# Dilated attention: the combination of the groups in five steps, each tied to a row minimum of the next items

## The chip, the cores and the metric

The kernel runs on one core of a Trainium2 chip. The metric is the device time of one execution in microseconds (us). The engines are TensorE (PE: matmuls and transposes), VectorE (DVE), ScalarE (ACT) and GpSimd (POOL); DMAs are issued from SyncE's queue (SP). Each engine takes its instructions in the order of its queue, and waits at one whose inputs or buffers are not ready.

## The reference, cut to what matters

The block has three attention mixers, whose outputs are gated, projected and merged. The change is in the first, dilated attention: 24 heads in three groups of eight, each group with its own window and dilation. Each group gives an output and a log-denominator per position and head, and a softmax over the three groups weighs the outputs:

```python
for gi, (window, dil) in enumerate(A_GROUPS):          # ((128, 1), (512, 4), (2048, 16))
    hs = slice(gi * A_HEADS, (gi + 1) * A_HEADS)
    o_g, lse_g = dilated_window_attention(aq[:, :, hs], ak[:, :, hs], av[:, :, hs], window, dil)
    outs.append(o_g)
    lses.append(lse_g)
wts = jax.nn.softmax(jnp.stack(lses, axis=0), axis=0).astype(dt)
oa = jnp.einsum('gbsh,gbshd->bshd', wts, jnp.stack(outs, axis=0)).reshape(b, s, BRANCH_WIDTH)
```

The sequence has 1024 positions, a head 64 channels.

## The kernel before

**Stages.** After the start come cross-attention, grouped-query attention, dilated attention (about 640 to 1165 us of the profiled span), the merge of the three branches, and the output projection. During the attentions PE also works through dense projections, one unit after the other (two halves of 24 matmuls, lines 143, 145 and 147). `weave` interleaves the matmuls of the attention with those of the units by their estimated costs, and PE's queue holds them as they are written. The other queues, SP's among them, are ordered by the recording layer, by priority and estimated readiness. The attention's instructions get a higher priority (`tc.high_priority`); the combination is traced outside of it.

**An item** is one pair of heads and one group. There are 12, in the order (0,0), (0,1), (0,2), (1,0) and so on; `a_att` computes one, in eight query tiles T = 0 to 7. A tile has these steps:

- scores on PE (line 125), into one of two PSUM banks;
- for each of the two heads the row minimum of the masked, negated scores, on DVE (line 939);
- the exponential on ACT (lines 942, 944, 947), into `pra`;
- two tiles later, the transposes of `pra` on PE (lines 965 and 974), into one of two PSUM banks `tr`, and their copy to `app` on ACT (line 977);
- after each four tiles, the matmuls with v (line 989) and the copy of the output to `og` on ACT (line 998). `og` has four buffers.

Meanwhile the dense units make q, k and v of the item after the next. Of each half of q and k, DVE makes three products with the rotary tables (lines 835 to 837) and POOL their sum (line 838, `rot`); then ACT and DVE split the result into a high and a low part: `aqh` (line 105) and `aql` (line 106) for q, `akh` (line 862) and `akl` (line 863) for k, head by head. POOL also copies edges of v (line 885, `vda`). Each unit's own weights arrive as `wr` (line 114, two buffers) and are split into `wh` on ACT (line 105) and `wl` on DVE (line 106).

**The combination** (`combine`) follows the third item of a pair. The statistics of the three groups were written to DRAM (`std`); two loads bring them back as `cpt` (line 1045). Seven small DVE operations and one exponential (lines 1047 to 1058) make the three weights of each position, `ceg`, which go to DRAM as `wgd` (line 1060). Then, for each group and each half of the positions, a pair of loads broadcasts the weights to 64 partitions each (`wgt`, line 1065, one buffer of 128x512), and DVE multiplies the output with them (line 1069). POOL adds the second and third output to the first (line 1071), and the sum goes to DRAM (`od`, line 1072).

The combinations of pairs 0, 1 and 2 run during the items (1,0), (2,0) and (3,0). That of pair 3 runs at the start of the merge, beside its units (line 1109 scales a unit, lines 1160 to 1163 prepare the gated outputs of the first branch, line 1125 accumulates). The merge loads the combined outputs for its third branch, and broadcasts the denominators of the second branch from DRAM with the same form of load (line 1141, 256 KB each, `gt`).

## Time and profile before

| | us |
|---|---|
| median of three runs | 1549.16 (1545.98 to 1551.1) |
| profiled execution | 1545.69 |
| its span, first to last instruction | 1543.9 |
| wgt loads in it (line 1065) | 48 of 128 KB, issued from 761.9 to 1212.5 |
| products with the weights (line 1069) | 24, median 1.09 each, from 766.2 to 1215.5 |
| additions on POOL (line 1071) | 8, median 2.40 each, from 782.4 to 1216.8 |

The profiled execution is 3.5 us shorter than the median of the runs; durations below come from it. A row of a timeline has the start from the span's start, the duration, the engine, the line, the operation, the tile written and the tiles read, and in brackets how long the engine stood idle before and what ended that. A row of waits has the total, the number of times and the longest.

### The profile page before, as it was taken

To read this page: it belongs to the slowest core of one execution; us is meant where nothing else is said; L and a number is where in the kernel's file an instruction comes from. 1 tells how busy PE (TensorE), PEld (TensorE's weight loads), DVE (VectorE), ACT (ScalarE), POOL (GpSimd) and SP (SyncE) were. 2 spreads that over 40 slices of the span, in tenths; PEclk is the share of its full clock that TensorE was granted. 3 is DMA by queue.
4 is the path that set the end of the run, shared out by engine and by line. 5 is a ranking of instruction groups with operands and counts; after the bars stand their busy time and mean duration, and the time that the engine had idled before them with its cause. 6 is when DMAs were issued, how large, how long until landed. Compare 5 with 4: busy or idle time off the path is not lost.

```text
span 1543.9 us, 20861 instructions
## 1 busy us (share of the span) xinstructions
PE 1497.0 (97%) x7748; PEld 1237.3 (80%) x7748; DVE 977.3 (63%) x1610; ACT 712.1 (46%) x1457; POOL 443.4 (29%) x363
## 2 busy tenths in 40 slices
PE   6999989999999999999999999999999999999998
PEld 5899977777777778888878877887888788888787
DVE  7765469989988975655566566556634442524743
ACT  5443345666677661645545445454643111212321
POOL 4415513454444543211231222123100100222422
PEclk9999999999999999999999999999999999999999
DMA  5342011111111112111120121112125451523432
GB/s 210 96 124 69 29 45 59 54 56 48 62 35 59 62 64 88 38 28 42 58 69 29 42 72 55 42 34 84 37 69 186 149 159 34 193 80 113 126 110 96
DMA packets 56966, 119.81 MB, mean 78 GB/s; under 512 B 14176, under 2 KB 24096, under 8 KB 56736
## 3 DMA queue, kind: packets, MB, share of 16 engines
q1 hardware_dynamic: 56720, 118.34, 23.8%
q8 instruction: 61, 1.00, 0.3%
q14 instruction: 41, 0.34, 0.1%
q10 hardware_dynamic: 144, 0.13, 0.0%
HBM read 96.06 MB, written 22.38 MB: 77 GB/s over the span
## 4 chain that ended last, share of the span: by engine, by line
PE 74%; DVE 12%; DMA 4%; issue 4%; ACT 3%; POOL 2%; SPq 1%; DVEq 0%; POOLq 0%; ACTq 0%
PE d L147 12%; PE d L143 12%; PE d L145 12%; PE sc L125 7%; PE sc L1226 4%; PE s L125 3%; PE sc L147 2%; PE sc L145 2%; PE sc L143 2%; PE ov L989 2%; DMA wgt<-wgd 2%; DVE bpl L106 2%; PE s L709 1%; PE ov L730 1%; PE s L708 1%
## 5 line engine op out<-in xcount | busy, mean ns | idle before, releaser
L143 PE MATMUL d<-hh,wh 128*128 128x512 f32 x992 | 396.0, 399 | 2.4 <-DVE fth L222 2.4
L147 PE MATMUL d<-hh,wl 128*128 128x512 f32 x992 | 397.3, 400 | 0.0
L145 PE MATMUL d<-hl,wh 128*128 128x512 f32 x992 | 393.6, 397 | 0.0
L143 PEld LDWEIGHTS d<-hh,wh 128*128 128x128 f32 x992 | 187.2, 189 | 39.2 <-DVE fth L222 3.2
L147 PEld LDWEIGHTS d<-hh,wl 128*128 128x128 f32 x992 | 187.1, 189 | 39.0 <-issue 4.1
L145 PEld LDWEIGHTS d<-hl,wh 128*128 128x128 f32 x992 | 187.3, 189 | 36.2 <-issue 1.0
L105 ACT ACTIVATE wh<-wr 128x1024 fp32r<-128x1024 f32 (+1 forms) x100 | 95.4, 954 | 242.9 <-PE sc L145 107.6
L838 POOL TENSOR_TENSOR rot<-rot,t2a 128x512 f32<-128x512 f32 x48 | 82.6, 1720 | 313.6 <-DVE t2a L837 313.6
L720 POOL TENSOR_TENSOR bl<-bl,bp 128x512 f32<-128x512 f32 x96 | 135.5, 1412 | 120.4 <-ACT bp L711 112.0
L106 DVE TENSOR_TENSOR bpl<-bp,bph 128x512 fp32r<-128x512 f32 x128 | 130.5, 1020 | 23.8 <-ACT bph L105 23.3
L106 DVE TENSOR_TENSOR wl<-wr,wh 128x1024 fp32r<-128x1024 f32 (+1 forms) x100 | 120.7, 1208 | 21.9 <-ACT wh L105 21.2
L711 ACT ACTIVATE bp<-s 128x512 f32<-128x512 f32 x128 | 76.2, 595 | 60.0 <-PE s L709 58.1
L1128 POOL TENSOR_TENSOR acc<-acc,th 128x1024 f32<-128x1024 f32 x16 | 45.4, 2836 | 192.7 <-DVE th L1127 192.7
L947 ACT ACTIVATE pra<-pra,sts 128x128 f32<-128x128 f32 (+2 forms) x152 | 67.1, 442 | 61.3 <-DVE sts L939 60.6
L147 PE MATMUL sc<-hh,wl 128*128 128x512 f32 x224 | 87.3, 390 | 2.3 <-DVE wl L106 2.3
L691 DVE TENSOR_REDUCE bn<-tr 128x1 f32<-128x512 f32 x128 | 86.6, 680 | 4.4 <-PE tr L690 4.0
L939 DVE CUSTOM_DVE_ANT_0 pra<-s,mask 128x128 f32<-128x128 f32 (+2 forms) x152 | 48.3, 348 | 62.3 <-PE s L125 50.1
L143 PE MATMUL sc<-hh,wh 128*128 128x512 f32 x224 | 87.3, 390 | 0.0
L145 PE MATMUL sc<-hl,wh 128*128 128x512 f32 x224 | 87.1, 389 | 0.0
L105 ACT ACTIVATE bph<-bp 128x512 fp32r<-128x512 f32 x128 | 80.8, 631 | 3.5
L835 DVE TENSOR_TENSOR rot<-d,tab 128x512 f32<-128x512 f32 x48 | 33.1, 690 | 73.3 <-PE d L147 73.1
L125 PE MATMUL sc<-gh,wh 128*128 128x512 f32 x192 | 74.7, 389 | 0.0
(278 smaller groups left out, 3097.2 us busy)
## 6 DMA issues: line engine op xcount, KB each, us to landing
wr<-in_wu SPq DMA_DIRECT2D x76, 512.0 KB
g2d<-fth SPq DMA_DIRECT2D x24, 256.0 KB
wgt<-wgd SPq DMA_DIRECT2D x48, 128.0 KB
ot<-od SPq DMA_DIRECT2D x12, 512.0 KB
gt<-g2d SPq DMA_DIRECT2D x12, 512.0 KB
wr<-in_wbr SPq DMA_DIRECT2D x24, 256.0 KB
thd<-fth SPq DMA_DIRECT2D x20, 256.0 KB
th<-thd SPq DMA_DIRECT2D x10, 512.0 KB
```

The lines of the kernel that those rows point to most:

```text
L105: A.activation(dst_h, src, AF.Copy)
L106: V.tensor_tensor(dst_l, src, dst_h.bitcast(F32), op=OP.subtract)
L125: PE.matmul(out_ps, a, b, start=i == 0, stop=i == n - 1)
L143: PE.matmul(dst, wh[:, k, :], hh[k][:, t], start=k == 0, stop=False)
L145: PE.matmul(dst, wh[:, k, :], hl[k][:, t], start=False, stop=False)
L147: PE.matmul(dst, wl[:, k, :], hh[k][:, t], start=False, stop=k == 7)
L691: V.tensor_reduce(st[i]["n"][:, j, c:c + 1], s, axis=AX.X, op=OP.min)
L711: A.activation(pp, s, AF.Exp, scale=-1.0)
L720: G.tensor_tensor(lsum[i % 2], lsum[i % 2], pp, op=OP.add)
L838: G.tensor_tensor(o[:, t], o[:, t], t2, op=OP.add)
L947: A.activation(src, raw, AF.Exp, scale=-1.0, bias=bias, accum_out=sts[:, h, 1, T:T + 1])
L1226: PE.matmul(parts[h], *terms[h][j], start=j == 0, stop=j == 23)
```

## The change

`combine` no longer issues its work at once. It returns five steps (the loads of the statistics; the weights, with their store and the first broadcast; one weighting per group), which are put on a list. In `a_att` of the following items, after the scores of tile T have been traced, the next step is traced if T is the step's number in `STEP_T`: 0, 2, 4 and 6 of the next item and 1 of the one after. `tc.issue_after` puts the step's DVE instructions behind that tile's last row minimum on DVE's queue; instructions of other engines are not bound. The steps are traced at the attention's priority.

The weight buffer `wgt` now holds 1024 positions, still one buffer: three pairs of loads of 256 KB and three products of 128x1024 per combination in place of six and six. Each load of the next group's weights stands directly behind the product that frees the buffer. The fourth combination runs its five steps one after the other, where it ran before. What is computed is the same.

```diff
@@ a_att
-            st = {}
+            st, last = {}, {}
...
-                    V.tensor_tensor_reduce(raw, sv[:, h], mask[:, mo:mo + n], 1.0, 3.0e38, OP.add, OP.min, bias)
+                    last["dve"] = V.tensor_tensor_reduce(raw, sv[:, h], mask[:, mo:mo + n], 1.0, 3.0e38, OP.add, OP.min, bias)
...
-                    yield scores(T)
+                    cost = scores(T)
+                    if todo and T == STEP_T[-len(todo)]:
+                        with tc.issue_after(last["dve"].ins):
+                            todo.pop(0)()
+                    yield cost
@@ combine
-            for g in range(3):
-                for e in range(2):
-                    wgt = cb.tile([P, 512], F32, name="wgt", bufs=1)
-                    for h in range(2):
-                        nc.sync.dma_start(wgt[h * 64:h * 64 + 64],
-                                          wgd[p_, h, g:g + 1, e * 512:e * 512 + 512].to_broadcast([64, 512]))
-                    wv = wgt.rearrange("p (b a) -> p a b", b=8)
-                    ogv = ogs[g].rearrange("p (a b) -> p a b", b=16)[:, :, e * 8:e * 8 + 8]
-                    V.tensor_tensor(ogv, ogv, wv, op=OP.mult)
-                if g:
-                    G.tensor_tensor(ogs[0], ogs[0], ogs[g], op=OP.add)
-            nc.sync.dma_start(od[0, p_], ogs[0])
+            def load(g):
+                wgt[g] = cb.tile([P, S], F32, name="wgt", bufs=1)
+                for h in range(2):
+                    nc.sync.dma_start(wgt[g][h * 64:h * 64 + 64], wgd[p_, h, g:g + 1].to_broadcast([64, S]))
+
+            def fetch():
+                c["t"] = cb.tile([P, 3, 2, 16], F32, name="cpt", bufs=1)
...
+            def weights():
+                cpt = c["t"]
...
+                load(0)
+
+            def weigh(g):
+                wv = wgt[g].rearrange("p (b a) -> p a b", b=16)
+                ogv = ogs[g].rearrange("p (a b) -> p a b", b=16)
+                V.tensor_tensor(ogv, ogv, wv, op=OP.mult)
+                if g < 2:
+                    load(g + 1)
+                if g:
+                    G.tensor_tensor(ogs[0], ogs[0], ogs[g], op=OP.add)
+                if g == 2:
+                    nc.sync.dma_start(od[0, p_], ogs[0])
+
+            return [fetch, weights] + [lambda g=g: weigh(g) for g in range(3)]
+
+        todo = []
+        STEP_T = (0, 2, 4, 6, 1)
@@ the loop over the items
-                combine(p_, [OG.pop((p_, x)) for x in range(3)])
+                todo += combine(p_, [OG.pop((p_, x)) for x in range(3)])
@@ the merge
-                        combine(3, [OG.pop((3, x)) for x in range(3)])
+                        for step in combine(3, [OG.pop((3, x)) for x in range(3)]):
+                            step()
```

More of the change, by code (lines that the diff above doesn't have):

```diff
@@ L1042, in combine @@
         def combine(p_, ogs):
-            cpt = cb.tile([P, 3, 2, 16], F32, name="cpt", bufs=1)
-            for h in range(2):
-                nc.sync.dma_start(cpt[h * 64:h * 64 + 64], std[p_, h].rearrange("g s (i e) -> i g s e", e=16))
-            mn = cb.tile([P, 16], F32, name="cmn", bufs=2)
-            V.tensor_tensor(mn, cpt[:, 0, 0], cpt[:, 1, 0], op=OP.min)
-            V.tensor_tensor(mn, mn, cpt[:, 2, 0], op=OP.min)
-            eg = cb.tile([P, 3, 16], F32, name="ceg", bufs=1)
-            V.tensor_tensor(eg, cpt[:, :, 0], mn[:, None, :].to_broadcast([P, 3, 16]), op=OP.subtract)
@@ L1051, in combine @@
-            A.activation(eg, eg, AF.Exp, scale=-1.0)
-            dn = cb.tile([P, 3, 16], F32, name="cdn", bufs=1)
-            V.tensor_tensor(dn, eg, cpt[:, :, 1], op=OP.mult)
-            ds_ = cb.tile([P, 16], F32, name="cds", bufs=2)
-            V.tensor_tensor(ds_, dn[:, 0], dn[:, 1], op=OP.add)
-            V.tensor_tensor(ds_, ds_, dn[:, 2], op=OP.add)
-            V.reciprocal(ds_, ds_)
-            V.tensor_tensor(eg, eg, ds_[:, None, :].to_broadcast([P, 3, 16]), op=OP.mult)
-            for h in range(2):
-                nc.sync.dma_start(wgd[p_, h].rearrange("g (i e) -> i g e", e=16), eg[h * 64:h * 64 + 64])
@@ L1061, in combine @@
-            for g in range(3):
-                for e in range(2):
-                    wgt = cb.tile([P, 512], F32, name="wgt", bufs=1)
-                    for h in range(2):
-                        nc.sync.dma_start(wgt[h * 64:h * 64 + 64],
-                                          wgd[p_, h, g:g + 1, e * 512:e * 512 + 512].to_broadcast([64, 512]))
-                    wv = wgt.rearrange("p (b a) -> p a b", b=8)
-                    ogv = ogs[g].rearrange("p (a b) -> p a b", b=16)[:, :, e * 8:e * 8 + 8]
-                    V.tensor_tensor(ogv, ogv, wv, op=OP.mult)
+            c = {}
@@ new lines, in combine @@
+            wgt = [None] * 3
+            def load(g):
[4 more added lines that the diff above has]
+                c["t"] = cb.tile([P, 3, 2, 16], F32, name="cpt", bufs=1)
+                for h in range(2):
+                    nc.sync.dma_start(c["t"][h * 64:h * 64 + 64], std[p_, h].rearrange("g s (i e) -> i g s e", e=16))
@@ new lines, in weights @@
+            def weights():
+                cpt = c["t"]
+                mn = cb.tile([P, 16], F32, name="cmn", bufs=2)
+                V.tensor_tensor(mn, cpt[:, 0, 0], cpt[:, 1, 0], op=OP.min)
+                V.tensor_tensor(mn, mn, cpt[:, 2, 0], op=OP.min)
+                eg = cb.tile([P, 3, 16], F32, name="ceg", bufs=1)
+                V.tensor_tensor(eg, cpt[:, :, 0], mn[:, None, :].to_broadcast([P, 3, 16]), op=OP.subtract)
+                A.activation(eg, eg, AF.Exp, scale=-1.0)
+                dn = cb.tile([P, 3, 16], F32, name="cdn", bufs=1)
+                V.tensor_tensor(dn, eg, cpt[:, :, 1], op=OP.mult)
+                ds_ = cb.tile([P, 16], F32, name="cds", bufs=2)
+                V.tensor_tensor(ds_, dn[:, 0], dn[:, 1], op=OP.add)
+                V.tensor_tensor(ds_, ds_, dn[:, 2], op=OP.add)
+                V.reciprocal(ds_, ds_)
+                V.tensor_tensor(eg, eg, ds_[:, None, :].to_broadcast([P, 3, 16]), op=OP.mult)
+                for h in range(2):
+                    nc.sync.dma_start(wgd[p_, h].rearrange("g (i e) -> i g e", e=16), eg[h * 64:h * 64 + 64])
+                load(0)
```

## The prediction

> **What bounds the kernel now.** I read the page's busy times first, then TensorE's waits over the stage of the dilated attention and its tail (640 to 1230 us from the span's start), then the timelines of the four compute engines around the longest of those waits.

> ```profile
> PE 1497.0 (97%) x7748; PEld 1237.3 (80%) x7748; DVE 977.3 (63%) x1610; ACT 712.1 (46%) x1457; POOL 443.4 (29%) x363
> ```

> TensorE (PE) is busy for 97% of 1543.9 us, so a saving has to be a gap on PE. The waits of PE between 640 and 1230 us (total us, times, longest us) name all there are, but for 0.3 us:

> ```profile
> PE tr L965 <- ACT app L977: 10.4, 3, 3.6
> PE sc L147 <- DVE wl L106: 2.3, 1, 2.3
> ```

> The three waits of 3.3, 3.6 and 3.5 us lie one in each of the first three combinations (for pairs 0, 1, 2), the 2.3 us in the fourth. 12.7 us is therefore the most that the change can give back in this stage. The first one, in the timelines (start, us, engine, line, operation; in brackets the idle time before and what ended it):

> ```profile
> 781.23 1.09 DVE L1069 TENSOR_TENSOR og<-og,wgt 128x512 f32<-128x512 f32 x1 [1.79 <-DMA wgt<-wgd]
> 782.35 0.69 DVE L836 TENSOR_TENSOR t2a<-d,tab 64x512 f32<-64x512 f32 x1
> 783.06 0.68 DVE L837 TENSOR_TENSOR t2a<-d,tab 64x512 f32<-64x512 f32 x1
> 783.77 2.11 DVE L106 TENSOR_TENSOR wl<-wr,wh 128x1024 fp32r<-128x1024 f32 x1
> ```
> ```profile
> 782.40 2.40 POOL L1071 TENSOR_TENSOR og<-og 128x1024 f32<-128x1024 f32 x1 [6.32 <-DVE og L1069]
> 784.76 2.27 POOL L838 TENSOR_TENSOR rot<-rot,t2a 128x512 f32<-128x512 f32 x1
> ```
> ```profile
> 787.07 2.13 ACT L862 ACTIVATE akh<-rot,cs 128x1024 fp32r<-128x1024 f32 x1 [7.43 <-POOL rot L838]
> ...
> 790.17 0.58 ACT L977 ACTIVATE app<-tr 128x512 f32<-128x512 f32 x1
> ```
> ```profile
> 790.81 0.55 PE L965 MATMUL tr<-cs,pra 128*128 128x128 f32 x3 [3.31 <-ACT app L977]
> ```

> Read it backwards. PE's last transposes wait for a PSUM bank that ScalarE (ACT) empties at 790.17. ACT stood 7.43 us in front of the split of k (akh), which needs the rotary sum on GpSimd (POOL, L838). POOL runs in order, and had the addition of two weighted outputs (L1071) ahead of it; that addition needed the fourth weighting product on VectorE (DVE) at 781.23, and this one its broadcast weights. The single weight buffer makes every product a round trip: the pair of loads is issued when the product before has ended, and the next product starts 3.4 to 3.8 us later (773.22 to 776.62, 777.70 to 781.23; in the tail 1192.52 to 1196.36). So the bound is a chain: DMA round trip, product, POOL, ACT, PE.

> **The change, part by part** (lines of the kernel before; the order on each queue is that of the changed kernel's own instructions).

> PE's order is the same. POOL's is the same where it matters: three rotary sums, the addition, then the fourth rotary sum. Only the second addition moves, into the next item. On DVE the eight small operations of the weights go behind the row minimum of tile 2; product 0 stands behind aql and ahead of tile 5's minima; product 1 behind those of tile 6; product 2 behind those of tile 1 of the next item. What is removed: 6 products of 128x512 and 12 loads of 128 KB per combination; added: 3 products of 128x1024 and 6 loads of 256 KB.

> *Price of a product.* Two halves took 2 x 1.05 to 1.09 us; aql, as strided and 128x1024, took 2.01. I take 2.12.

> *Price of a load pair (L, from the end of the product before to the start of the next).* The nearest row is the merge's broadcast of the same 2 x 256 KB from one row of DRAM to 64 partitions each:

> ```profile
> 1233.02 1.09 SPq L1141 DMA_DIRECT2D gt<-rld  x2
> ```
> ```profile
> 1237.78 1.23 DVE L1142 TENSOR_TENSOR ot<-ot,gt 128x1024 f32<-128x1024 f32 x1 [2.52 <-DMA gt<-rld]
> ```

> That is 4.76 us; the other three took 4.80, 5.34 and 5.06, all four beside other loads. The lower end is the half-sized pair's 3.4. I take 4.76, since nothing else moves between 772 and 778 us now. [...]

> *Weights.* Tile 2's minima end near 759.05 once nothing stands before them. cmn, cmn, ceg (0.17, 0.18, 0.21), ACT's exponential (0.23), then 0.21, 0.17, 0.17, 0.25, 0.21 with gaps end at 761.3 instead of 759.96. The write of wgd takes 1.9 us until the loads are issued (759.99 to 761.89), so wgt 0 is issued at 763.2 and lands at about 768.0. The next minima (761.59) aren't touched: nothing.

> *Product 0.* aql ends at 770.93, 2.9 us after the landing: no wait. It ends at 773.05. Behind it are tile 5's minima, now 2.2 us later (before: 770.85). Then exp (two of 0.49) and the copy app give 775.0; the PV matmuls that need it start on PE at 776.07. Cover: 1.07 us. Tile 6 is 1.1 us later, with over 6 us to spare (784 us).

> *Product 1.* 773.05 + 4.76 = 777.8; DVE is free from 776.55, waits, and ends at 779.93. Behind it are the three rotary products of k's second half (0.69, 0.69, 0.68): 782.0, where they ended at 783.74 before. POOL's addition: 780.0 to 782.4. Then DVE's wl (1.23 alone, 2.11 beside POOL) and POOL's sum (1.3 alone, 2.27 beside DVE) share about 2.4 us, as before, wl first: the sum ends at 784.85. ACT's akh starts at 784.9 in place of 787.07: **2.2 us earlier**. The rest of the chain (3.74 us from akh to the transposes) is unchanged, so 3.3 us of wait become 1.1. Bounds: L = 3.4 gives 776.55 for the product, and nearly the whole wait goes (3.3); L = 5.34 gives 1.6.

> [...]

> *Product 2* at tile 1 of the next item: 809.5 to 811.6. Its weights were issued at 780. Behind it tile 2's minima go from 810.58 to 811.65, the rotary sum from 814.20 to 814.65, wl's end (816.5 now) to about 817.0, needed at the unit's change near 821. POOL was idle from 807.7 to 814.2 and takes the addition at 811.6. SP's queue: the store of the outputs stands ahead of one weight load, but that load waits for wl at about 817 anyhow. Cost: nothing; without this cover 1 us of DVE.

> *Fourth combination.* The 2.27 us went because wl (1217.64) stood on DVE behind the sixth product (1215.50). Three round trips end at about 1208 instead of 1216.6, so this wait goes. A new one comes: product 1 now is ahead of the th and wl that PE needs at 1201.52. Product 0 ends at 1193.54; L here is 4.76 to 5.34 (a store of weights lies beside it; this place's small pair took 3.84 against 3.4), I take 5.1: 1198.6, + 2.12, + th 1.14, + wl 1.2 = 1203.1. New wait 1.6, net **0.7** (0.5 to 2.0). Wl of the branch weights at 1195.35 instead of 1193.1 is still ahead of its matmul (1196.08).

> Sum: 3 x 2.2 + 0.7 = 7.3, and 0.3 as the second wait was 0.3 longer for a slower load: **7.6 us**, with bounds 3 x 1.6 + 0.5 = 5.3 and 10.4 + 2.0 = 12.4. Behind the stage PE is the bound again (1.1 us of waits from 1221 to the merge's end), so the saving stays. The profiled execution took 1545.69 us (span 1543.9): 1538.1. The three timed runs have a median of 1549.16, 3.5 above it; I state the forecast against that median: 1541.6.

> **The rivals.**

> *All of the waits go* (L near 3.4, or POOL's sum ahead of wl): 12.4 off, 1536.8. For it: the quiet DMA at 772 to 778 us. Against: four rows of equal size, none under 4.76.

> *Within 0.3%* (4.6 us, about what a measurement of this kernel can tell from no change). POOL keeps its order, so the tie itself frees nothing there; all hangs on L. At L = 6.0 each combination gives 1.0, the fourth nothing: 3 us off, 1546. At 7.0 the product is where it was.

> *Slower.* Product 0 stands in front of tile 5's minima. Had wgt 0 not landed when DVE arrives, DVE's whole queue would stand, and with it exp, app and PE's PV matmuls, whose cover is 1.07 us. Its loads lie beside a 512 KB load (766 to 771 us, DMA up to 0.91 busy). A delay of s costs PE s - 1.07 there and takes 1.07 of the 2.2 later: even at s = 2.2, that is a landing at 773.1, 9.9 us after the issue. At s = 4.3, three times 2.1 us are lost, less 0.7: 5.6 slower, 1555. Against it: the longest load that the chain of waits names in this stage, 512 KB, took 6.72 us.

> **Chances.** Forecast (5.3 to some 10 off) 0.62; all goes 0.08; within 0.3% 0.19; slower 0.11. So faster 0.70, same 0.19, slower 0.11. The range: 1536.5 (all goes) to 1547.5, which leaves out the slower rival and the weakest of the third.

> **What would show it.** Right: PE's wait for app falls from 10.4 to about 3.5 us; POOL's first addition starts some 2.4 us earlier against the scores of tile 7; DVE waits about 1.2 us for wgt ahead of product 1 and none ahead of 0 and 2; PE's wait for wl moves to the third unit of the merge, 1 to 2 us. Wrong: a new PE wait at the PV matmuls (product 0), or for scores in the item behind (product 2), or L far from 4.76.

## The result, and the profile after

The changed kernel took 1534.84 us (median of five runs, 1533.89 to 1537.39), the kernel before, run beside it, 1547.50 (1544.43 to 1551.1): a ratio of 0.9923, interval 0.9906 to 0.9941, or 12.7 us less (9.1 to 14.5). Run again later it gave 1537.14 against 1548.97, 0.9927 (0.9913 to 0.9942), 11.8 us less. The forecast was 7.6 us less (1541.6 us, in a range from 1536.5 to 1547.5). The changed kernel's profiled execution took 1537.39 us, span 1535.6.

The page's busy times, and PE's waits from 640 to 1230 us (total us, times, longest us):

```profile
PE 1498.6 (98%) x7748; PEld 1238.4 (81%) x7748; DVE 972.8 (63%) x1598; ACT 712.7 (46%) x1457; POOL 443.9 (29%) x363
```
```profile
PE tr L965 <- ACT app L977: 1.9, 3, 0.7
PE sc L147 <- DVE wl L106: 1.8, 1, 1.8
PE ov L989 <- ACT app L977: 0.8, 3, 0.3
```

Before, the same three rows held 10.4, 2.3 and 0.3, 13.0 in all; now they hold 4.5. **8.5 us of waits went.** The first combination, from the timeline of all engines (this execution is 1.0 us late at this point: the copy `sr` ahead of it starts at 748.42 in place of 747.42):

```profile
778.48 2.04 DVE L1083 TENSOR_TENSOR og<-og,wgt 128x1024 f32<-128x1024 f32 x1 [1.13 <-DMA wgt<-wgd]
...
780.60 2.41 POOL L1087 TENSOR_TENSOR og<-og 128x1024 f32<-128x1024 f32 x1 [2.63 <-DVE og L1083]
...
782.56 1.53 DVE L106 TENSOR_TENSOR wl<-wr,wh 128x1024 fp32r<-128x1024 f32 x1
...
782.96 2.28 POOL L838 TENSOR_TENSOR rot<-rot,t2a 128x512 f32<-128x512 f32 x1
...
785.28 2.16 ACT L862 ACTIVATE akh<-rot,cs 128x1024 fp32r<-128x1024 f32 x1 [4.64 <-POOL rot L838]
...
789.05 0.55 PE L965 MATMUL tr<-cs,pra 128*128 128x128 f32 x3 [0.55 <-ACT app L977]
```

It is the chain of the kernel before, link by link, but with two round trips less ahead of it: the product that POOL's addition needs is the second of three, not the fourth of six. The addition comes 2.8 us earlier (780.60 less 1.0, against 782.40), akh 2.8 us earlier, and PE waits 0.55 in place of 3.31.

So much was forecast, nearly. But 8.5 us of waits aren't 12.7. The rest is in **the granted clock** (TensorE's clock as a share of its full speed). Windows of 1 us in the kernel before, behind PE's wait of 3.59 us (columns: window, its length, busy time of PE, PEld, DVE, ACT and POOL with instructions, TensorE's granted clock, DMA share, GB/s):

```profile
929.00:930.00 1.00, 1.00 (x5) 0.90 (x6) 1.00 (x3) 1.00 (x1) 0.00 (x0) 0.62 0.01 4
930.00:931.00 1.00, 1.00 (x5) 0.35 (x5) 0.50 (x1) 1.00 (x2) 0.39 (x1) 0.50 0.08 16
931.00:932.00 1.00, 1.00 (x12) 1.00 (x14) 1.00 (x1) 0.84 (x2) 0.40 (x1) 0.50 0.00 0
932.00:933.00 1.00, 1.00 (x16) 1.00 (x14) 1.00 (x1) 0.00 (x0) 0.00 (x0) 0.67 0.00 0
933.00:934.00 1.00, 1.00 (x16) 0.79 (x11) 1.00 (x2) 0.28 (x1) 0.00 (x0) 1.00 0.00 0
```

The clock drops to 0.50 for 3.4 us (929.24 to 932.65) just after PE works again at 928.96; PE shows 100% busy through it, so no view of busy times or waits has this loss. In PE's timeline of the changed kernel the same happens behind its wait for wl; matmuls of one size take 0.63 us, and 0.40 once it is over:

```profile
1193.84 0.50 PE L147 MATMUL sc<-hh,wl 128*128 128x512 f32 x1 [1.80 <-DVE wl L106]
...
1194.94 0.63 PE L147 MATMUL sc<-hh,wl 128*128 128x512 f32 x1
...
1198.28 0.40 PE L147 MATMUL sc<-hh,wl 128*128 128x512 f32 x1
```

In the stage the profile of before has two such stretches (929, 1069), that of after one (1194), and none behind its waits of 0.55 to 0.73. What one costs comes from the `sr` copies, one pair of heads apart. Before: 137.85, 139.26 and 139.17 us, with waits of 3.31, 3.59 and 3.46 in them, the first without a stretch. Less what the waits differ, 139.26 - 137.85 - 0.28 = 1.1 us, and 139.17 - 137.85 - 0.15 = 1.2.

The timed executions of before, by their clock, have more of it than the profiled one: their mean clocks are 0.987 to 0.993 (median 0.991 or 0.990 in each group of runs) and go with the time (1553.23 us at 0.987, 1545.34 at 0.992); the profiled one had 0.993. The changed kernel's runs have 0.993 to 0.996.

### The profile page after: what moved, and what is told of

Same layout as the page of the kernel before. It is cut to its first block, busy times and chain, and to the rows that moved or that the text cites. A ratio compares the mean times of both kernels' runs of the same rounds, so it can differ in the third digit from the quotient of the medians.

```text
span 1535.6 us, 20807 instructions
## 1 busy us (share of the span) xinstructions
PE 1498.6 (98%) x7748; PEld 1238.4 (81%) x7748; DVE 972.8 (63%) x1598; ACT 712.7 (46%) x1457; POOL 443.9 (29%) x363
## 4 chain that ended last, share of the span: by engine, by line
PE 75%; DVE 11%; issue 4%; ACT 3%; DMA 3%; POOL 2%; SPq 0%; DVEq 0%; POOLq 0%; ACTq 0%
PE d L147 12%; PE d L143 12%; PE d L145 12%; PE sc L125 7%; PE sc L1248 4%; PE s L125 3%; PE sc L147 3%; PE sc L145 3%; PE sc L143 3%; PE ov L989 2%; DVE bpl L106 2%; PE s L709 1%; DVE bn L691 1%; PE ov L730 1%; PE s L708 1%
## 5 line engine op out<-in xcount | busy, mean ns | idle before, releaser
L147 PE MATMUL d<-hh,wl 128*128 128x512 f32 x992 | 397.2, 400 | 0.0
L147 PEld LDWEIGHTS d<-hh,wl 128*128 128x128 f32 x992 | 187.1, 189 | 38.5 <-issue 3.6
L838 POOL TENSOR_TENSOR rot<-rot,t2a 128x512 f32<-128x512 f32 x48 | 82.6, 1721 | 297.4 <-DVE t2a L837 297.4
L106 DVE TENSOR_TENSOR bpl<-bp,bph 128x512 fp32r<-128x512 f32 x128 | 130.5, 1020 | 23.8 <-ACT bph L105 23.3
L106 DVE TENSOR_TENSOR wl<-wr,wh 128x1024 fp32r<-128x1024 f32 (+1 forms) x100 | 119.0, 1191 | 21.2 <-ACT wh L105 20.5
L147 PE MATMUL sc<-hh,wl 128*128 128x512 f32 x224 | 87.8, 392 | 1.8 <-DVE wl L106 1.8
```

Of the source, the lines that this page charges most:

```text
L106: V.tensor_tensor(dst_l, src, dst_h.bitcast(F32), op=OP.subtract)
L147: PE.matmul(dst, wl[:, k, :], hh[k][:, t], start=False, stop=k == 7)
L838: G.tensor_tensor(o[:, t], o[:, t], t2, op=OP.add)
```

## The experiments

Two theories. **A**: a wait of PE costs its length and, in many executions, a stretch at half clock behind it, so that 8.5 us of waits shorter give some 12. **B**: a wait costs its length alone, and the rest came from elsewhere. Beside these, the parts of the change (wide buffer, five places, tie) are taken apart. The table has them all. "Waits" is PE's total in the stage from each profile, "work" what extra matmuls were put in, "less" 13.0 minus both, and "faster" the difference of medians, each to the runs of before beside it.

| run | waits | work | less | faster | ratio (interval) | median clock |
|---|---|---|---|---|---|---|
| before_again | 13.5 | | -0.5 | -1.5 | 1.0004 (0.9994-1.0015) | 0.991 |
| after_again | 4.4 | | 8.6 | 11.8 | 0.9927 (0.9913-0.9942) | 0.994 |
| width_only | 9.3 | | 3.7 | 5.5 | 0.9962 (0.995-0.9975) | 0.993 |
| untied | 7.9 | | 5.1 | 8.7 | 0.9948 (0.9936-0.9959) | 0.993 |
| halves_tied | 26.0 | | -13.0 | -15.0 | 1.0093 (1.0079-1.0108) | 0.989 |
| late_product | 2.2 | | 10.8 | 15.5 | 0.9899 (0.9885-0.9912) | 0.996 |
| half_buffers | 0.8 | | 12.2 | 17.1 | 0.9891 (0.9876-0.9906) | 0.995 |
| half_late | 0 | | 13.0 | 20.3 | 0.9869 (0.9856-0.9881) | 0.996 |
| busy_wait | 1.5 | 8.2 | 3.3 | 5.6 | 0.9957 (0.9943-0.9971) | 0.994 |
| filled_wait | 5.8 | 8.2 | -1.0 | 3.2 | 0.9979 (0.9969-0.9988) | 0.995 |
| order_only | 8.6 | 0.7 | 3.7 | 4.8 | 0.9969 (0.9955-0.9983) | 0.993 |

Read the last columns together: where the clock is above before's 0.990 or 0.991, the kernel is faster than the waits say (by 1 to 7 us), and where it is below, slower by 2.

**before_again**: the kernel before, unchanged.

> The kernel before, unchanged, in other executions. Theory A (waits and clock): a PE wait of some 2 to 4 us is followed, in part of the executions, by about 3.5 us in which the granted clock is 0.5, which costs 1 to 2 us more; the waits themselves are the same in each execution (three of 3.3 to 3.6 us, one of 2.3). Then the profile has the same four waits within 0.3 us, a granted clock of 0.5 behind some of them, perhaps others than in the first profile, and the times of the executions go with their mean granted clock (0.001 of it for each spell, 1 to 2 us). Theory B (round trips): the clock is no part; the broadcasts take longer in some executions, and the waits of this profile differ from those of the first by over 1 us. Ratio 1.000 to 0.002.

Its profile has the waits again (3.51, 3.78, 3.38 and 2.47), and stretches behind the second and third wait, as in the first profile. The ratio is within its interval of 1.

**width_only**: the old place and order, the buffer of 1024.

```diff
-                for e in range(2):
-                    wgt = cb.tile([P, 512], F32, name="wgt", bufs=1)
...
+                wgt = cb.tile([P, S], F32, name="wgt", bufs=1)
```

> The combination untied and at its old place, with the weight buffer of 1024 alone (three round trips for six). On DVE's queue the products 0 and 1 then stand where the change has them; product 2 stands ahead of wl and of tile 7's minima, and waits there for its weights. If the ties matter by what they move (product 2), each of the three waits falls from about 3.4 to about 2.5 us, and the fourth as in the change: 2 to 5 us faster than before. If width is all that matters, the waits fall to 0.6 as in the change, 9 to 13 us faster.

The waits for app are 1.86, 1.93 and 2.49, the wait for wl 2.42: the buffer alone takes off about half of what the change takes off the waits for app (4.1 of 8.5 us). Half-clock stretches lie behind the waits of 1.86 and 2.42, and none behind 1.93 and 2.49.

**untied**: the change, with the steps traced at their five places but not bound.

```diff
-                        with tc.issue_after(last["dve"].ins):
-                            todo.pop(0)()
+                        todo.pop(0)()
```

> The changed kernel with its five steps at the same places of the program but without the tie to the row minima, so that VectorE's order is the scheduler's. If the five places alone make the gain: as the change, waits for app of 0.5 to 0.8 us, ratio 0.992. If the tie is needed as well: the products slip among other work, waits for app of 1.9 to 2.5 us as in the run that has the wide buffer alone, ratio 0.995 to 0.997.

The waits for app are 2.09, 1.95 and 2.20. DVE's timeline of it shows why:

```profile
779.81 2.04 DVE L1082 TENSOR_TENSOR og<-og,wgt 128x1024 f32<-128x1024 f32 x1 [1.34 <-DMA wgt<-wgd]
...
786.43 2.05 DVE L1082 TENSOR_TENSOR og<-og,wgt 128x1024 f32<-128x1024 f32 x1 [2.58 <-DMA wgt<-wgd]
788.39 1.22 DVE L106 TENSOR_TENSOR wl<-wr,wh 128x1024 fp32r<-128x1024 f32 x1
789.53 0.35 DVE L939 CUSTOM_DVE_ANT_0 pra<-s,mask 128x192 f32<-128x192 f32 x1
```

Left free, product 2 goes ahead of wl and of tile 7's minima, and DVE stands 2.58 us for its weights; in the changed kernel it follows in the next item, at 807.60, and the minima come at 784.18. So the tie is worth 1.1 to 1.5 us at each wait, by keeping product 2 back.

**halves_tied**: the tied steps with the old buffer, six round trips.

```diff
-                wgt[g] = cb.tile([P, S], F32, name="wgt", bufs=1)
+                wgt[g] = cb.tile([P, 512], F32, name="wgt", bufs=1)
...
+                for e in range(2):
+                    if e:
+                        load(g, e)
```

> The changed kernel's five tied steps with the old single buffer of 512: each product is again two halves with a round trip of 3.4 to 3.5 us between. The width theory (the gain comes from fewer round trips): the fourth half-product ends at about 783 against 781 us, and the loads between hold VectorE's queue; akh starts near 790, the waits for app grow to about 6 us, 8 to 10 us slower than before, ratio 1.005 to 1.007. The tie theory (the gain comes from where the products stand on VectorE's queue): waits for app below 2 us and faster than before, ratio 0.995 to 0.997.

```profile
PE tr L965 <- ACT app L977: 15.2, 3, 5.1
PE s L125 <- ACT pra L944: 5.0, 3, 1.7
PE d L143 <- DVE t2a L837: 4.0, 3, 1.5
PE sc L147 <- DVE wl L106: 1.8, 1, 1.8
```

The width theory holds, and the loss is larger than it said (15.0 us): akh starts at 790.96 and each wait for app is 5.1, a little less than expected, but the products that wait on DVE's queue also hold up its rotary products (PE waits for t2a up to 1.5 us) and, in the next item, the scores (1.7). **The tie without short round trips was a loss here**: DVE stood 1.70, 1.94 and 2.35 us for weights ahead of the three half-products from 775.92 to 785.24, with whatever stands behind them on its queue.

**late_product**: the fourth step at tile 7.

```diff
-        STEP_T = (0, 2, 4, 6, 1)
+        STEP_T = (0, 2, 4, 7, 1)
```

> The change with product 1 tied to tile 7 in place of tile 6. POOL's queue then has the fourth rotary sum ahead of the addition. If the remaining wait of 0.6 us in each of the three combinations is the addition standing ahead of that sum (2.4 us on POOL) and the DMA round trip ahead of it, it goes to 0 to 0.2 us, and the kernel is 1 to 2 us faster than the change (11 to 15 faster than before). If something else ends last there, the waits stay at 0.6.

POOL's fourth rotary sum now comes ahead of the addition, no wait for app is left, and the only wait of the stage is for wl (2.2). No half-clock stretch lies in the stage.

**half_buffers**: two buffers of 512, the half for the next group loaded as soon as its buffer is free.

```diff
-                wgt[g] = cb.tile([P, S], F32, name="wgt", bufs=1)
+                wgt[g, e] = cb.tile([P, 512], F32, name="wgt", bufs=2)
...
+                for e in range(2):
...
+                    if g < 2:
+                        load(g + 1, e)
```

> The change with two weight buffers of 512 in place of one of 1024 (same memory; six loads pairs, six products of half size), each next half fetched while the other half is multiplied. It takes away the wait for the round trip ahead of product 1 (1.1 to 1.4 us of DVE) without moving anything else. If L is the term that is left, POOL's addition and akh start 1.1 to 1.3 us earlier, the waits of 0.6 go to 0 to 0.1; in the fourth combination product 1's wait of 2.8 falls to about 1.8 and PE's wait for wl from 1.8 to about 0.8 us. In all 2.5 to 3.5 us faster than the change, and up to 2 more where its wl wait drew a spell of half clock. If small products cost more than the round trip gives, no faster than the change.

DVE doesn't wait for weights in the items: product 1 starts at 776.67. In the fourth combination its halves wait 0.94 and 0.59 us where the wide product waited 2.82, so that the wait for wl goes too.

**half_late**: both together.

> Two 512 buffers with the next half loaded ahead, the five steps tied, and the fourth step at tile 7 in place of 6 (the candidate for the fastest version). Either theory: no PE wait over 0.3 us in the first three combinations and in the fourth; clock 0.995 to 0.997. By the 0.28 us of waits for PV that the run with two buffers still had three times, 0.8 us less than it: ratio 0.988 to 0.989, about 1530. If the halves now come too late for akh, a wait for app of 0.5 us comes back and the ratio is 0.990.

No wait of PE is left in the stage and none appears elsewhere; this is the fastest version, 1529.06 us (1528.62 to 1529.88). On DVE the two halves of product 0 run back to back, without a wait (771.14 to 773.22), and those of product 1 start at 784.15, behind tile 7's minima.

**busy_wait**: the kernel before with 12 matmuls whose results are never read, ahead of the transposes that wait.

```diff
+                if T - LA_T == NT - 1 and g == 0 and p_ > 0:
+                    spare = pso()
+                    for _ in range(12):
+                        PE.matmul(spare, qh[:, 0:128], kh[:, 0, 0:512], start=True, stop=True)
```

> The kernel before, with 12 extra matmuls of 128x512 (about 2.7 us of TensorE work, results never read) put ahead of the last transposes of the first three combinations' items, where PE waits 3.3 to 3.8 us. The chain that ends the wait isn't touched. Theory A (a wait costs its length, and in most executions a stretch of 3.4 us at half clock behind it): the waits for app shrink from 3.5 to about 0.8 us each, the transposes start when they did, no half-clock stretch lies behind them, mean clock up by 0.002; 2.5 to 4.5 us faster than before although PE does more, ratio 0.997 to 0.9985. Theory B (a wait costs its length alone, and what the change gave beyond 8.5 us came from elsewhere): the same time or up to 1.5 us slower, ratio 1.000 to 1.001.

Faster by 5.6 us with 8.2 us more of PE work. But the matmuls read akh, so ACT's next akh came behind them and behind app: the waits for app went altogether, and the run doesn't tell the theories apart. Two runs take its two effects one by one.

**filled_wait**: the same matmuls, on operands that nothing waits for.

```diff
-                        PE.matmul(spare, qh[:, 0:128], kh[:, 0, 0:512], start=True, stop=True)
+                        PE.matmul(spare, hh[0][:, 0:128], hh[0][:, 0:512], start=True, stop=True)
```

> The kernel before with the 12 extra matmuls of 128x512 at the same three places, but reading only the hidden rows (hh), so that nothing waits for them and ACT, DVE, POOL and SP keep their orders word for word (in the run before this one they read the old akh, and ACT's next akh came behind them and behind app). The wait for app therefore ends when it did in the kernel before, with 0.5 to 0.9 us of idle left of it. Theory A (behind a wait there is, in most executions, a stretch at half clock): no such stretch behind the three, mean clock up by 0.001 to 0.003, 2 to 4.5 us faster, ratio 0.997 to 0.9987. Theory B (a wait costs only its length): ratio 1.000 to 1.001.

PE's timeline at the second wait, and the clock behind it:

```profile
925.41 2.89 PE L1007 MATMUL ov<-hh 128*128 128x512 f32 x12
929.11 0.55 PE L965 MATMUL tr<-cs,pra 128*128 128x128 f32 x3 [0.81 <-ACT app L977]
```
```profile
929.00:934.00 5.00, 4.59 (x44) 3.55 (x45) 4.45 (x5) 3.60 (x5) 0.79 (x2) 1.00 0.00 0
```

The transposes start when they did (929.11 here, 928.96 before), the wait is now filled with useless work, and the clock stays at 1.00 where it averaged 0.66 over the same 5 us. PE gains nothing by the work, and yet the median of the timed runs is **3.2 us lower**, at a clock of 0.995 for 0.990, with an interval that excludes 1. Theory A holds; B doesn't. The one profiled execution shows less: its span is 1544.0, against 1543.9 and 1544.4 of before. The pairs of heads with a stretch are shorter (138.12 for 139.26, 138.39 for 139.17), but the first, which had none to lose, is 0.6 longer, as its chain ended 0.5 us later, and a stretch, at 1219.6, lies behind this execution's wait for wl (2.03 us), where before had none behind its 2.27 us; and what the timed executions of before have beyond two stretches isn't in a profile.

**order_only**: one such matmul in place of twelve, reading akh, so that only ACT's order changes (and DVE's v copy comes ahead of akl).

```diff
-                    for _ in range(12):
+                    for _ in range(1):
```

> The kernel before with one extra matmul (0.23 us on PE, result never read) at those three places that reads the old akh, so that ACT's next akh comes behind app; DVE's v copy (vta) then comes ahead of akl. The combination isn't touched. If the wait for app is there only because app stands behind akh on ACT's queue: the three waits go as in the changed kernel, 10 us and the half-clock stretches less, ratio 0.990 to 0.993 (as the change). If akh's lateness costs PE elsewhere (k's split is needed by the next item's scores): a wait for akl or vta of 1 to 3 us appears and the ratio is 0.996 or more.

The waits don't go; 1.97, 2.42 and 2.12 are left. The timeline of all engines:

```profile
784.04 2.10 DVE L106 TENSOR_TENSOR wl<-wr,wh 128x1024 fp32r<-128x1024 f32 x1
...
786.34 1.87 DVE L1073 TENSOR_TENSOR og<-og,wgt 128x512 f32<-128x512 f32 x1
788.14 0.35 DVE L939 CUSTOM_DVE_ANT_0 s<-s,mask 128x192 f32<-128x192 f32 x1
...
788.64 0.37 ACT L942 ACTIVATE pra<-s,sts 128x128 f32<-128x128 f32 x1 [1.58 <-DVE sts L939]
...
789.28 1.08 ACT L977 ACTIVATE app<-tr 128x512 f32<-128x512 f32 x2
```

With akh out of its way, app stands behind tile 7's exponentials, these behind the minima, and these behind wl and the fifth half-product on DVE. My expectation had seen one cause where there were two in a row: the second was 1.3 us behind the first. The change shortens the first (akh starts 2.8 us earlier) and takes the second away (tile 7's minima end before 785.0, ahead of akh), as its products stand elsewhere on DVE's queue.

**after_again**: the changed kernel, unchanged.

> The changed kernel unchanged, beside the same runs of the kernel before: ratio 0.991 to 0.994; which of its waits draw a half-clock stretch may differ from its first profile.

Waits of 0.90, 0.82, 0.73 and, for wl, 1.11; no stretch at half clock in the stage; span 1533.9.

## Why the prediction was wrong, point by point

**The step that failed** is the price of a wait in the sum, and what was laid on top of the sum: "12.7 us is therefore the most that the change can give back in this stage", and then "3.5 above it; I state the forecast against that median". Each wait was priced at its length, with nothing for the clock behind it, and the 3.5 us between the profiled execution and the median was taken as a constant. Neither holds: half_late, which has no wait left, is 15.8 us shorter by the profiled spans (1543.9 to 1528.1; 13.0 of waits, and 2.3 for two stretches) and 20.3 by the medians. A wait also drew a stretch at half clock, often, but not each time; the profiled execution of before was one with few of them, the median, by its clock, had more, and they went with the waits. Against profiled executions the forecast is near: 1545.69 - 7.6 = 1538.1, and 1537.39 was measured, in an execution that was the slowest of its five. The size: filled_wait takes the stretches behind the three waits for app away and leaves the chain, and gives 3.2 us; 8.5 + 3.2 = 11.7, against 12.7 and 11.8 measured. (PE's waits and extra work there are 1.0 us longer than the waits before, so the clock alone may have given 4.2.) By profile pairs: before_again (two stretches, waits 13.5) to after_again (none, 4.4) is 9.1 of waits and 1544.4 - 1533.9 = 10.5 of span.

The profile could have told, though not by its page, whose clock row has a 9 (90% or more) in each of its 40 slices: windows of 1 us behind the 3.59 us wait show 0.50. I read the 97% of PE as 97% at full speed. A wait needn't be that long: waits of 1.80 us (for wl, in the changed kernel), 1.86 (the first of width_only) and 2.03 (for wl, in filled_wait) had a stretch of 3.4 us behind them too.

**Which waits draw a stretch.** The clock records of the thirteen traces tell it. In each execution the recorded clock changes only at the ends of windows of 3.413 us, which follow one another without a gap through the span and lie differently in different executions (an end at 929.24 in the profile of before, at 928.02 in that of after). From 64 us on, the clock was halved behind each of the 28 windows at full clock in which PE's idle time came to 1.86 us or more, and behind none of the 5497 with 1.78 or less; of the five between, two were followed by a stretch. So in these traces a wait counts by the part of it that falls into one window. In the kernel before, the end of a window cut the first wait (787.50 to 790.81) in two, and nearly all of the second (925.37 to 928.96) fell into one (columns as in the windows above):

```profile
785.89:789.30 3.41, 1.61 (x10) 1.04 (x7) 2.48 (x6) 2.23 (x2) 1.14 (x1) 1.00 0.47 156
789.30:792.71 3.41, 1.90 (x20) 1.49 (x22) 3.04 (x3) 3.41 (x8) 0.31 (x1) 1.00 0.24 79
925.83:929.24 3.41, 0.28 (x3) 0.29 (x4) 2.47 (x4) 3.41 (x9) 0.00 (x0) 1.00 0.52 185
```

That leaves 1.80 and 1.51 us of idle time in the first two windows, and the clock stayed; 3.13 in the third, and the clock fell at its end. An estimate from this: with the windows laid at every place over PE's waits in the stage, and 1.82 us as the bound, before has 2 to 4 stretches, 3.4 on average, the changed kernel none or one, filled_wait 0.5 on average. The profiled execution of before, with two, was thus among the lowest, and about three went with the change: at 1.1 to 1.2 us each some 3.5 us, where the measurements exceed the waits by 4.2 (12.7 less 8.5) and 2.7 (11.8 less 9.1).

**L and the first product.** Forecast 4.76, measured 4.63 (773.85, the end of product 0, to 778.48). Product 0 had no wait, as forecast; DVE waited 1.13 us ahead of product 1 (forecast 1.2).

**Each combination, 2.2 forecast.** The waits for app fell by 2.8 on average. The 0.6 us more are small parts of one sign, in the first combination, with 1.0 taken off this execution's times: product 1 0.3 earlier (777.5 for 777.8) and 0.1 shorter (2.04 for 2.12), addition and sum together 4.6 for 4.85. Against it stand 0.5 us of new waits for the matmuls with v (0.3 to 0.8), behind the last transposes of an item. That wl stands ahead of the sum and both share the time was right: wl from 782.56, 1.53 us, the sum from 782.96, 2.28 us.

**Product 2 at tile 1**: 807.60 to 809.6, no wait behind it that PE shows. Right.

**Fourth combination, 0.7 forecast**: the old wait for wl (2.27) went and a new one came, as said, 1.80 us (forecast 1.6), later 1.11; net 0.5 and 1.2. The new one drew a stretch in the first profile, and the rest of the span, from the last `sr` copy on, was 1.3 us longer than before, though its wait was 0.5 shorter; in after_again, without a stretch, it was 1.0 shorter.

**Rivals.** "All of the waits go" named 1536.8, close to the time measured, for another reason: 4.5 us of waits are left, so that its nearness is luck. "Within 0.3%" hung on L at 6.0 or more, and L was 4.63. "Slower" didn't come; untied and halves_tied show that its mechanism (DVE held by a load, with the rest of its queue behind) is real: DVE stood 2.58 us in the one, up to 2.35 us in the other.

**Still open**: whether the stretches behind these waits account for it all. The medians of clock differ by 0.005 between before and filled_wait, or 7 us of full-clock time in 1549, which is four stretches of 3.4 us (1.7 us lost in each), for three filled waits, or 2.9 stretches by the estimate. Some may be longer (the one at the first 5.08 us wait of halves_tied began in the wait and took 7 us). Each profile also has stretches outside of the stage, near 38 and 220 us, of 3.4 or 6.8 us each, and one at the end, whatever the kernel; the timed executions have no trace to show theirs.

## What to carry to other kernels

Where TensorE is the bound, price its wait at its length and what its clock does behind it: here 1.1 to 1.2 us for each stretch, unseen in busy shares; look at the granted clock in 1 us windows behind every wait, and compare the mean clock of the profiled execution with those of the timed ones before taking their difference as constant. The single buffer fed by DMA made a round trip of each use, 3.4 to 3.5 us for 2 x 128 KB and 4.63 for 2 x 256 KB in the first combination: use fewer, larger loads, or two buffers of half the size, which cost the same memory and gave some 5 us more than the wide one. And before one queue's order is blamed for a wait, look at what the waiting instruction would stand behind next.
